# A hybrid encoder block on one core: attention values of two heads per 512-column product, and the recurrence's second output product issued earlier

## The chip, the cores and the metric

The kernel runs on one core of a Trainium2 chip. The time is the device time of one execution in microseconds (us); the median of several executions is the figure that counts. Everything is float32; TensorE does most products on float32 values split into a high and a low part.

## The reference

One layer of a trunk in which a differential attention and an RWKV-7 recurrence read the same normalised input and are merged by gates. 256 rows, width 2048, one layer:

```
h    = rmsnorm(x)
proj = h @ W_in                                  # q, k, v | r, k, v, low-rank columns | gate logits
A    = diff_attention(q, k, v)                   # 8 heads, each 2 x 128 for q and k, 256 for v
         p = softmax(q0 k0) - lam * softmax(q1 k1);  o = p @ v;  o = rmsnorm(o)
Bm   = rwkv7(...)                                # 32 heads of 64, per step:
         sa = state @ a;  state = state * w + sa b^T + v k^T;  y = state @ r
mix  = (sigmoid(gA) * (A @ W_a) + sigmoid(gB) * (Bm @ W_b)) @ W_out
x    = x + rmsnorm(mix)
x    = x + rmsnorm(swiglu(rmsnorm(x)))           # 2048 -> 2 x 5632 -> 2048
```

## The kernel before

Weights come from HBM in units of 128 x 1024 float32 (512 KB). `unit_parts` (lines 108 to 116) loads one into a `raw` tile (four buffers, issued on SP's queue), ACT copies it to a rounded high part `hi` (line 115), DVE subtracts to get the low part `lo` (line 116); `hi` and `lo` have four buffers each. `project_t` makes 128 output columns transposed, with the weights stationary: per 128 input columns one product of 512 columns (high weights, line 128) and one of 256 (low weights, line 131); ACT and DVE then add the two halves (`total`, lines 138 and 139). `project_rows` (lines 163 to 194) keeps the activations stationary and streams the weights: three products (high x high, high x low, low x high, line 177) per 128 input columns and per half of the 256 rows.

The first stage interleaves 16 groups of two recurrence heads (`rwkv_prep(g)`, lines 450 to 563) with 8 attention heads (`attention(h)`, lines 565 to 630) in the sequence `ORDER` (line 19): items 0 to 15 are groups, 100 to 107 are attention heads, and the list ends with 14, 15, 106, 107. A list scheduler with a simulated timeline then places each instruction on its engine's queue, so the written sequence is only a start; each queue runs strictly in its order.

`attention(h)` projects two q and two k parts with `project_t`, then the values of this head (256 columns): four units of weights, 96 products of 256 columns into one PSUM bank `va` whose two halves are the two row halves. ACT copies the bank to `vs[0]`, DVE subtracts to get `vs[1]` (lines 582 and 583). The scores (line 590) go to `mm` banks, softmax runs on ACT and DVE in a tile `pe`, line 605 transposes it, and line 613 multiplies by the values. PSUM has three `acc`, three `mm` and two `tr` banks.

`rwkv_prep(g)` ends with small products for a chunk's matrices (line 541, into two `mm` banks, read by DVE in line 544), and stores them to DRAM (`img`, `tl`). DVE then inverts 64 x 64 triangular matrices of eight groups at once (lines 390 to 396), which sit in `arena`: `inv_load(p)` (lines 384 to 388) is four loads from POOL's queue, each 8 rows of 16 KB (`arena<-tl`), and `inv_store` (lines 404 to 407) is two stores of 256 KB (`tx<-arena`). Loads for pair p = 4 and p = 5 are issued behind a step of groups 14 and 15; loads for p = 6 and p = 7 are issued behind the last q/k step of attention head 6 (lines 642 to 645).

Later, while the gate logits, `A @ W_a` and `Bm @ W_b` run, the recurrence proper is done in `chunk(p, c, ...)` (lines 696 to 736): 8 pairs p of groups times 4 chunks c. Each chunk has four small products per step, two heads into an `mm` bank and two into a `tr` bank, one on the upper and one on the lower 64 partitions: line 706 (full array), line 717 (64 x 64), line 723 (the next state's product), line 732 (the second part of the output Y). Between 717 and 723 DVE copies the state (720); behind 723 DVE adds or copies the next state from the bank (728, 730); behind 732 ACT copies Y out (736). In the profile each of these float32 products shows as two records.

Of the kernel before, what the change touches and what calls it, by code (L numbers as in the profile page):

```python
# [67 lines left out]
def hybrid_block(ctx: ExitStack, tc: tile.TileContext, io):  # L68
# [91 lines left out]
                    step_t(out, hi, lo, kk, xT, u * 8 + kk, nk)  # L160
        return [total(out) for out in outs]

    def project_rows(outs, src, base, xT, nk, width, banks_shared=False, tail=0):

        per = 1024 // width
        n = nk // per

        def part(u, j, hi, lo):
            for kk in range(per):
                k = u * per + kk  # L170
                wh, wl = hi[:, kk * width:(kk + 1) * width], lo[:, kk * width:(kk + 1) * width]
                for jj in j:
                    xh = xT[:, k, jj * P:(jj + 1) * P]
                    xl = xT[:, k, T + jj * P:T + (jj + 1) * P]
                    for i, (x, w) in enumerate(((xh, wh), (xh, wl), (xl, wh))):
                        first = k == 0 and i == 0 and (jj == 0 or not banks_shared)
                        mm = nc.tensor.matmul(outs[jj], lhsT=x, rhs=w, start=first,  # L177
                                              stop=(k == nk - 1 and i == 2 and (jj == 1 or not banks_shared)))
            return mm

        held = []
        for u in range(n):
            hi, lo = unit(src[base + u])
            if u < n - tail:
                mm = part(u, (0, 1), hi, lo)
            else:
                held.append((u, hi, lo))
        if tail:
            for u, hi, lo in held:
                mm = part(u, (0,), hi, lo)  # L190
            with tc.issue_after(mm.ins):
                for u, hi, lo in held:
                    mm = part(u, (1,), hi, lo)
        return mm
# [142 lines left out]
    with tc.tile_pool(name="hpool", bufs=1) as hpool:  # L337
# [42 lines left out]
        lt = arena[:, 0:4096].rearrange("p (s t) -> p s t", s=CH)  # L380
        xt = arena[:, 4096:6144].rearrange("p (j t) -> p j t", j=32)
        tmi = arena[:, 6144:7168]

        def inv_load(p):

# [23 lines left out]
        with tc.tile_pool(name="att", bufs=2) as w2, tc.tile_pool(name="mix1", bufs=2) as w1:  # L409
# [40 lines left out]
            def rwkv_prep(g):  # L450
# [111 lines left out]

                return after_kq, after_bkp

            def attention(h):
                def tmp(tag, shape=(P, T), bufs=2):
                    return w2.tile(list(shape), F32, tag=tag, name=tag, bufs=bufs)
                qk = []
                for i in range(4):
# [6 lines left out]
                    t = tmp(f"qk{i}", bufs=1)  # L576
                    after_qk = nc.gpsimd.tensor_tensor(out=t, in0=m1, in1=m2, op=ALU.add)
                    qk.append(t)
                va = bank("acc")
                project_rows([va[:, 0:256], va[:, 256:512]], io["w_inv"], 4 * h, hT, NK, 256, banks_shared=True)  # L580
                vs = [w2.tile([P, 2 * T], F32R, tag=f"vs{i}", name=f"vs{i}", bufs=1) for i in range(2)]
                nc.scalar.copy(vs[0], va)
                nc.vector.tensor_tensor(out=vs[1], in0=va, in1=vs[0].bitcast(F32), op=ALU.subtract)
                ptp = bank("tr")
                for qt in range(2):
                    nk = P * (qt + 1)
# [5 lines left out]
                    mx = tmp("mx", (P, 2))  # L592
                    nc.vector.tensor_reduce(out=mx, in_=s, axis=AX.X, op=ALU.max)
                    nc.vector.tensor_scalar(out=mx, in0=mx, scalar1=-SCALE, scalar2=None, op0=ALU.mult)
                    pe = tmp("pe", (P, 2, 256))
                    z = tmp("z", (P, 2))
                    for c in range(2):
                        nc.scalar.activation(pe[:, c, 0:nk], s[:, c], AF.Exp, scale=SCALE, bias=mx[:, c:c + 1], accum_out=z[:, c:c + 1])
# [11 lines left out]
                for q, pairs in enumerate(([(0, 0)], [(1, 0), (2, 1)])):  # L610
                    terms = [(a, b, i, j) for i, j in pairs for a, b in ((0, 0), (0, 1), (1, 0))]
                    for n, (a, b, i, j) in enumerate(terms):
                        nc.tensor.matmul(ob[:, q * T:(q + 1) * T], lhsT=pT[a][:, i * P:(i + 1) * P], rhs=vs[b][:, j * T:(j + 1) * T],
                                         start=(n == 0), stop=(n == len(terms) - 1))
                os_ = tmp("os", (P, 2, 256))
                ss = tmp("oss", (P, 2))
# [78 lines left out]
        with tc.tile_pool(name="chain", bufs=2, reuse_waits="tile") as cp:  # L695
            def chunk(p, c, ck, tb, y, nxt):
# [24 lines left out]
                if nxt is not None:  # L721
                    for g, h, o in heads:
                        nc.tensor.matmul(banks[h][own[h], 2 * P + o:2 * P + o + CH], lhsT=ckh[:, g, h, BKC:UVC], rhs=ckh[:, g, h, UVC:HW],
                                         start=True, stop=True, skip_group_check=True)
                    for h in range(2):
                        new = nxt[:, :, 0:ARC].rearrange("p g (h w) -> p g h w", h=2)[own[h], :, h, UVC:HW]
                        if c:
                            nc.vector.tensor_tensor(out=new, in0=part(banks[h][own[h]], 2), in1=st[own[h]], op=ALU.add)
                        else:
                            nc.vector.tensor_copy(new, part(banks[h][own[h]], 2))  # L730
                for g, h, o in heads:
                    nc.tensor.matmul(banks[h][own[1 - h], o:o + CH], lhsT=ck[own[h], g, ARC:IW], rhs=ckh[own[h], g, h, UVC:HW],  # L732
                                     start=False, stop=(g == 1), skip_group_check=True)
                yh = y[rows, c // 2].rearrange("p (g h e) -> p g h e", g=2, h=2)
                for h in range(2):
                    nc.scalar.copy(yh[:, :, h], part(banks[h][own[1 - h]], 0))
# [173 lines left out]
def prepare(x, w_in, b_gate, g_mix_pre, g_mix_post, g_ffn_pre, g_ffn_post, da_lambda_q, da_lambda_k, da_subln_g,  # L910
# [12 lines left out]
    for h in range(NH):  # L923
# [17 lines left out]
        "cst": _constants(),  # L941
        "vec": a(vec),
        "w_inb": a(_units_t(np.concatenate(cols, axis=1))),
        "w_inv": a(_units_rows(w[:, 4096:6144], 256)),
        "up_wa": a(np.concatenate([wu, au], axis=2).transpose(1, 0, 2)),
        "up_g": a(gu.transpose(2, 1, 0, 3).reshape(NG, P, 2 * P)),
        "w_ba": a(_units_t(np.asarray(w_branch_a)[0])),
# [21 lines left out]
```

## Time and profile before

| | |
|---|---|
| runs | 1996.11 us median of three (1995.98, 1996.11, 3871.28) |
| the profiled execution's own time | 1993.32 us |
| its span, first to last instruction | 1991.5 us |
| TensorE products (PE) busy | 1963.0 us, 99% |
| TensorE weight loads busy | 1698.6 us, 85% |
| DVE, ACT, POOL busy | 1354.0, 1026.3, 266.6 us |
| moved by DMA | 401.44 MB, mean 202 GB/s |

The stages follow one another: normalisation up to 25 us, recurrence preparation and attention up to about 680, gate logits, branch products and the recurrence up to 1153, `W_out` up to 1240, then the feed-forward layer. Busy time of PE is a modelled one for pipelined products, so what a product costs is read from the distance between starts.

### The profile page before, as it was taken

What the parts mean: (1) busy time and instruction counts of PE and PEld (TensorE: products, weight loads), DVE (VectorE), ACT (ScalarE), POOL (GpSimd) and SP (SyncE); (2) the same over time, 40 slices, a digit from 0 to 9 for tenths busy, and PEclk for the clock granted to TensorE, in tenths of its full rate; (3) what the DMA queues carried; (4) which work ended last, traced back from release to release, by engine and by line L of the source; (5) the groups of instructions that cost most, each with busy time, mean ns of one, the idle gap of its engine ahead of it and who ended that gap; (6) DMA issues with size and microseconds to landing.
All of it is one profiled execution on the core that took longest, in us unless ns stands there. A gap on an engine that the chain in (4) does not pass through costs nothing.

```text
span 1991.5 us, 32080 instructions
## 1 busy us (share of the span) xinstructions
PE 1963.0 (99%) x11934; PEld 1698.6 (85%) x11934; DVE 1354.0 (68%) x2173; ACT 1026.3 (52%) x1861; POOL 266.6 (13%) x359
## 2 busy tenths in 40 slices
PE   9999999999998999999999999999999999999998
PEld 8898899888887888888888888888888888888886
DVE  6767777899986888756656755656565656544444
ACT  6655655656664544445444444644444444434442
POOL 0224224133245111221110000000000000000000
PEclk9999999999999999999999999999999999999999
DMA  7677777765679675667546575555555555555664
GB/s 249 207 209 216 217 207 225 197 204 188 205 226 214 191 248 191 219 223 252 195 153 207 192 254 190 166 188 188 189 189 190 190 189 188 189 195 192 193 195 140
DMA packets 139307, 401.44 MB, mean 202 GB/s; under 512 B 32784, under 2 KB 45328, under 8 KB 138128
## 3 DMA queue, kind: packets, MB, share of 16 engines
q1 hardware_dynamic: 116432, 346.95, 54.5%
q0 software_dynamic: 12864, 45.10, 7.5%
q10 hardware_dynamic: 9856, 7.34, 1.2%
q8 instruction: 94, 1.54, 0.3%
q14 instruction: 61, 0.50, 0.1%
HBM read 368.92 MB, written 30.41 MB: 201 GB/s over the span
## 4 chain that ended last, share of the span: by engine, by line
PE 85%; DVE 6%; DMA 4%; issue 3%; ACT 1%; POOL 1%; DVEq 0%; SPq 0%; POOLq 0%; ACTq 0%
PE acc L128 39%; PE acc L131 20%; PE acc L177 18%; DMA raw<-w_inb 2%; DVE lo L116 2%; PE mm L206 1%; PE mm L706 1%; DVE arena L394 1%; PE tr L706 1%; DVE arena L396 1%; ACT hi L115 1%; PE mm L128 1%; PE mm L541 0%; PE tr L732 0%; PE tr L717 0%
## 5 line engine op out<-in xcount | busy, mean ns | idle before, releaser
L116 DVE TENSOR_TENSOR lo<-raw,hi 128x1024 fp32r<-128x1024 f32 x624 | 774.2, 1242 | 502.5 <-ACT hi L115 498.5
L115 ACT ACTIVATE hi<-raw 128x1024 fp32r<-128x1024 f32 x623 | 660.0, 1060 | 757.2 <-issue 313.8
L128 PE MATMUL acc<-hT,hi 128*128 128x512 f32 x1840 | 594.3, 400 | 0.0
L128 PE MATMUL acc<-h2T,hi 128*128 128x512 f32 x1392 | 439.3, 396 | 0.0
L131 PEld LDWEIGHTS acc<-hT,lo 128*128 128x128 f32 x1840 | 342.8, 188 | 76.7 <-DVE lo L116 1.6
L131 PE MATMUL acc<-hT,lo 128*128 128x256 f32 x1840 | 381.4, 284 | 0.6 <-DVE lo L116 0.5
L131 PEld LDWEIGHTS acc<-h2T,lo 128*128 128x128 f32 x1392 | 261.2, 188 | 60.6
L128 PEld LDWEIGHTS acc<-hT,hi 128*128 128x128 f32 x1840 | 285.6, 189 | 3.1 <-ACT hi L115 0.3
L131 PE MATMUL acc<-h2T,lo 128*128 128x256 f32 x1392 | 274.8, 278 | 0.0
L177 PE MATMUL acc<-hi,f 128*128 128x512 f32 x704 | 216.8, 389 | 0.0
L128 PEld LDWEIGHTS acc<-h2T,hi 128*128 128x128 f32 x1392 | 213.2, 189 | 0.8
L177 PEld LDWEIGHTS acc<-hi,f 128*128 128x128 f32 x704 | 132.2, 188 | 27.4
L177 PE MATMUL acc<-lo,f 128*128 128x512 f32 x352 | 136.9, 389 | 0.0
L229 POOL TENSOR_TENSOR rlastq<-rlast,mhalf 128x1 f32<-128x1 f32 x8 | 4.8, 606 | 942.5 <-DVE rlast L227 751.2
L139 DVE TENSOR_TENSOR sum<-acc,sum 128x256 f32<-128x256 f32 x233 | 97.3, 418 | 0.8
L177 PE MATMUL acc<-hi,hT 128*128 128x256 f32 x512 | 94.3, 283 | 0.0
L138 ACT COPY sum<-acc 128x256 f32<-128x256 f32 x233 | 83.7, 359 | 1.0 <-PE acc L128 0.3
L128 PE MATMUL acc<-oaT,hi 128*128 128x512 f32 x256 | 82.8, 399 | 0.0
L177 PEld LDWEIGHTS acc<-hi,hT 128*128 128x128 f32 x512 | 80.4, 191 | 0.0
L177 PE MATMUL acc<-hi,mixT 128*128 128x512 f32 x256 | 79.0, 389 | 0.0
L177 PEld LDWEIGHTS acc<-lo,f 128*128 128x128 f32 x352 | 66.1, 188 | 13.7
L128 PE MATMUL acc<-obT,hi 128*128 128x512 f32 x240 | 76.0, 395 | 0.0
(251 smaller groups left out, 2272.5 us busy)
## 6 DMA issues: line engine op xcount, KB each, us to landing
raw<-w_f SPq DMA_DIRECT2D x264, 512.0 KB, 3.5
raw<-w_inb SPq DMA_DIRECT2D x232, 512.0 KB, 4.1
ck<-img POOLq DMA_DIRECT2D x32, 576.0 KB, 5.9
raw<-w_inv SPq DMA_DIRECT2D x32, 512.0 KB, 4.0
raw<-w_ba SPq DMA_DIRECT2D x32, 512.0 KB, 3.6
raw<-w_bb SPq DMA_DIRECT2D x32, 512.0 KB, 3.5
raw<-w_out SPq DMA_DIRECT2D x32, 512.0 KB, 4.1
img<-stg POOLq DMA_DIRECT2D x32, 256.0 KB, 4.4
```

What stands on the lines that cost most here:

```text
L115: return (hi, lo, lambda: nc.scalar.activation(hi, raw, AF.Copy), lambda: nc.vector.tensor_tensor(out=lo, in0=raw, in1=hi.bitcast(F32), op ...
L116: lambda: nc.vector.tensor_tensor(out=lo, in0=raw, in1=hi.bitcast(F32), op=ALU.subtract), raw)
L128: nc.tensor.matmul(out, lhsT=hi[:, kk * P:(kk + 1) * P], rhs=xT[:, k, :], start=(k == 0), stop=(k == nk - 1))
L131: nc.tensor.matmul(out[:, 0:T], lhsT=lo[:, kk * P:(kk + 1) * P], rhs=xT[:, k, 0:T], start=False, stop=False)
L138: nc.scalar.copy(t, out[:, T:2 * T])
L139: nc.vector.tensor_tensor(out=t, in0=out[:, 0:T], in1=t, op=ALU.add)
L177: mm = nc.tensor.matmul(outs[jj], lhsT=x, rhs=w, start=first, stop=(k == nk - 1 and i == 2 and (jj == 1 or not banks_shared)))
L206: nc.tensor.matmul(out, lhsT=w[:, i:i + P], rhs=x, start=(n == 0), stop=(n == len(terms) - 1))
L229: nc.gpsimd.tensor_tensor(out=q, in0=r, in1=mhalf[:, 0:1], op=ALU.pow)
L394: nc.vector.tensor_tensor(out=tv, in0=xt[:, 0:n, s:s + 1].to_broadcast([P, n, m]), in1=lt[:, s:s + 1, s + 1:CH].to_broadcast([P, n, m]), o ...
L396: nc.vector.tensor_tensor(out=xt[:, 0:n, s + 1:CH], in0=xt[:, 0:n, s + 1:CH], in1=tv, op=ALU.add)
L706: nc.tensor.matmul(banks[h][:, o:o + CH], lhsT=ckh[:, g, h, 0:P], rhs=ckh[:, g, h, UVC:HW], start=(g == 0), stop=(g == 1))
```

## The change

Values: `attention(h)` projects values only when h is even, then for heads h and h + 1 together. The weights `w_inv` are laid out in units of 2 x 512 columns instead of 4 x 256, the two row halves take one `acc` bank each, and a product has 512 columns. The parts live in four tiles `vs00` to `vs11` until head h + 1 has used them. To make room, the softmax tile `pe` becomes a slice of `arena` (columns 7168 to 8191, otherwise unused). The argument `banks_shared` goes.

Recurrence: in `chunk`, the four products of the second part of Y (line 732 before, 730 after) are written directly behind the next state's products (723 before, 727 after), ahead of DVE's reading of that state.

```diff
-    def project_rows(outs, src, base, xT, nk, width, banks_shared=False, tail=0):
+    def project_rows(outs, src, base, xT, nk, width, tail=0):
...
-                        first = k == 0 and i == 0 and (jj == 0 or not banks_shared)
-                        mm = nc.tensor.matmul(outs[jj], lhsT=x, rhs=w, start=first,
-                                              stop=(k == nk - 1 and i == 2 and (jj == 1 or not banks_shared)))
+                        mm = nc.tensor.matmul(outs[jj], lhsT=x, rhs=w, start=(k == 0 and i == 0), stop=(k == nk - 1 and i == 2))
...
+        probs = arena[:, 7168:8192].rearrange("p (q c k) -> p q c k", q=2, c=2)
...
+            values = {}
...
-                va = bank("acc")
-                project_rows([va[:, 0:256], va[:, 256:512]], io["w_inv"], 4 * h, hT, NK, 256, banks_shared=True)
-                vs = [w2.tile([P, 2 * T], F32R, tag=f"vs{i}", name=f"vs{i}", bufs=1) for i in range(2)]
-                nc.scalar.copy(vs[0], va)
-                nc.vector.tensor_tensor(out=vs[1], in0=va, in1=vs[0].bitcast(F32), op=ALU.subtract)
+                if h % 2 == 0:
+                    va = [bank("acc"), bank("acc")]
+                    project_rows(va, io["w_inv"], 4 * h, hT, NK, 512)
+                    for j in range(2):
+                        values[j] = [w2.tile([P, 2 * T], F32R, tag=f"vs{j}{i}", name=f"vs{j}{i}", bufs=1) for i in range(2)]
+                        nc.scalar.copy(values[j][0], va[j])
+                        nc.vector.tensor_tensor(out=values[j][1], in0=va[j], in1=values[j][0].bitcast(F32), op=ALU.subtract)
...
-                    pe = tmp("pe", (P, 2, 256))
+                    pe = probs[:, qt]
...
-                        nc.tensor.matmul(ob[:, q * T:(q + 1) * T], lhsT=pT[a][:, i * P:(i + 1) * P], rhs=vs[b][:, j * T:(j + 1) * T],
+                        nc.tensor.matmul(ob[:, q * T:(q + 1) * T], lhsT=pT[a][:, i * P:(i + 1) * P], rhs=values[j][b][:, h % 2 * T:(h % 2 + 1) * T],
...
+                for g, h, o in heads:
+                    nc.tensor.matmul(banks[h][own[1 - h], o:o + CH], lhsT=ck[own[h], g, ARC:IW], rhs=ckh[own[h], g, h, UVC:HW],
+                                     start=False, stop=(g == 1), skip_group_check=True)
+                if nxt is not None:
                     for h in range(2):
...
                         else:
                             nc.vector.tensor_copy(new, part(banks[h][own[h]], 2))
-                for g, h, o in heads:
-                    nc.tensor.matmul(banks[h][own[1 - h], o:o + CH], lhsT=ck[own[h], g, ARC:IW], rhs=ckh[own[h], g, h, UVC:HW],
-                                     start=False, stop=(g == 1), skip_group_check=True)
...
-        "w_inv": a(_units_rows(w[:, 4096:6144], 256)),
+        "w_inv": a(_units_rows(w[:, 4096:6144], 512)),
```

The first place is TensorE's queue (PE) in the recurrence, early in the second pair's chunks; L128 and L131 are products of the large projections that run at the same time, `mm` and `tr` the two banks of a chunk. Before:

```order
L723 MATMUL mm<-ck 64x64 x2
L128 MATMUL acc<-hT,hi 128x512
L131 MATMUL acc<-hT,lo 128x256 x2
L128 MATMUL acc<-hT,hi 128x512 x2
L131 MATMUL acc<-hT,lo 128x256 x2
L128 MATMUL acc<-hT,hi 128x512 x2
L131 MATMUL acc<-hT,lo 128x256 x2
L732 MATMUL mm<-ck 64x64 x2
L732 MATMUL tr<-ck 64x64 x2
L706 MATMUL mm<-ck 128x64 x2
L723 MATMUL tr<-ck 64x64 x2
```

The same stretch of PE's queue after the change, where L727 is the next state's product and L730 the second part of Y:

```order
L128 MATMUL acc<-hT,hi 128x512 x2
L727 MATMUL mm<-ck 64x64
L727 MATMUL tr<-ck 64x64
L727 MATMUL mm<-ck 64x64
L727 MATMUL tr<-ck 64x64
L730 MATMUL mm<-ck 64x64
L730 MATMUL tr<-ck 64x64
L730 MATMUL mm<-ck 64x64
L730 MATMUL tr<-ck 64x64
```

The second part of Y left its own gaps between the large products and stands behind the state's products, with the two banks in turn. Over the whole queue the number of unbroken stretches that hold any of the 64 x 64 products falls from 101 to 68, and the number of groups of one line within them from 125 to 122.

The second place is POOL's queue at groups 14 and 15 and attention head 6. `arena<-tl` are the loads for the inversion (four to a pair p), `kq` and `bkp` steps of a group, `qk` the last step of a q or k part, `tx` the stores of the inverse. Before, from group 15's `kq` on:

```order
L496 TENSOR_TENSOR kq<-kr,mhalf 128x4
L388 DMA arena<-tl_85 8x4096 x4
L577 TENSOR_TENSOR qk_7495<-m_7490,m_7492 128x256
L388 DMA arena<-tl_85 8x4096 x4
L528 DMA bv_d<-sq 128x256
L517 TENSOR_TENSOR bkp<-bk,pt 128x512
L407 DMA tx_86<-arena 32x2048 x2
```

After, from group 14's second q/k step to group 15's loads:

```order
L527 DMA bv_d<-sq 128x256
L579 TENSOR_TENSOR qk_7195<-m_7190,m_7192 128x256
L387 DMA arena<-tl_85 8x4096 x4
L516 TENSOR_TENSOR bkp<-bk,pt 128x512
L406 DMA tx_86<-arena 32x2048 x2
L555 DMA img_83<-stg 64x4x64 x2
L559 DMA img_83<-stg 64x4x256
L560 DMA img_83<-stg 64x4x128
L559 DMA img_83<-stg 64x4x256
L560 DMA img_83<-stg 64x4x128
L495 TENSOR_TENSOR kq<-kr,mhalf 128x4
L387 DMA arena<-tl_85 8x4096 x4
```

The loads of p = 6 moved from behind those of p = 5 (one q/k step apart) to ahead of group 14's stores, so that the stores and a step of group 15 lie between the two sets of loads.

## Rows read from the trace of the kernel before

**Rows 1.** The page, its first part: busy time of each engine.

```profile
PE 1963.0 (99%) x11934; PEld 1698.6 (85%) x11934; DVE 1354.0 (68%) x2173; ACT 1026.3 (52%) x1861; POOL 266.6 (13%) x359
```

**Rows 2.** Busy time by stretch, columns in the first row.

```profile
core 0: us, PE busy (x) PEld busy (x) DVE busy (x) ACT busy (x) POOL busy (x), PEclk, DMA share, GB/s
...
600.00:680.00 80.00, 68.37 (x468) 62.15 (x467) 54.88 (x102) 34.36 (x68) 33.90 (x47) 0.94 0.86 208
...
860.00:960.00 100.00, 99.80 (x723) 82.50 (x722) 61.16 (x116) 52.68 (x116) 18.30 (x25) 1.00 0.67 225
```

**Rows 3.** The chain that ended last: start, us, what, number of products.

```profile
103.00 11.51 PE acc L177 x96
...
1153.93 72.10 PE acc L177 x318
```

**Rows 4.** Groups of line 177 in the value projections, by line.

```profile
L177 PE MATMUL acc<-hi,hT 128*128 128x256 f32 x512 | 94.3, 283 | 0.0
...
L177 PE MATMUL acc<-lo,hT 128*128 128x256 f32 x256 | 72.9, 285 | 0.0
```

**Rows 5.** Timeline of PE, 600 to 690: start, us, what, idle before and its releaser.

```profile
633.54 0.40 PE L131 MATMUL acc<-hT,lo 128*128 128x256 f32 x2
642.59 2.07 PE L590 MATMUL mm<-qk,qk 128*128 128x256 f32 x4 [8.65 <-DVE stg L544]
644.10 1.41 PE L128 MATMUL acc<-hT,hi 128*128 128x512 f32 x2
...
648.08 0.63 PE L128 MATMUL acc<-hT,hi 128*128 128x512 f32 x2
```

**Rows 6.** Timelines of DVE, ACT and POOL, 612 to 646.

```profile
640.71 1.23 DVE L116 TENSOR_TENSOR lo<-raw,hi 128x1024 fp32r<-128x1024 f32 x1 [10.61 <-ACT hi L115]
641.85 1.28 DVE L544 TENSOR_TENSOR stg<-mm,cst 128x512 f32<-128x512 f32 x2
...
639.62 1.06 ACT L115 ACTIVATE hi<-raw 128x1024 fp32r<-128x1024 f32 x1 [11.71 <-DMA raw<-w_inb]
...
617.01 2.10 POOL L388 DMA_DIRECT2D arena<-tl  x4
...
622.17 2.02 POOL L388 DMA_DIRECT2D arena<-tl  x4
```

**Rows 7.** The chain that ended last, 600 to 690.

```profile
621.67 17.85 DMA raw<-w_inb
```

**Rows 8.** DMA issues of the whole span: KB each, median us to landing.

```profile
raw<-w_inb SPq DMA_DIRECT2D x232, 512.0 KB, 4.1
...
arena<-tl POOLq DMA_DIRECT2D x32, 128.0 KB, 10.1
```

**Rows 9.** Timeline of PE in the recurrence, 722 to 760.

```profile
721.86 0.63 PE L128 MATMUL acc<-hT,hi 128*128 128x512 f32 x2
...
724.65 0.63 PE L128 MATMUL acc<-hT,hi 128*128 128x512 f32 x2
...
741.55 0.39 PE L128 MATMUL acc<-hT,hi 128*128 128x512 f32 x1
741.87 0.45 PE L723 MATMUL tr<-ck 128*64 128x64 f32 x4
742.24 0.44 PE L717 MATMUL tr<-w,tb 64*64 64x64 f32 x4
...
742.96 0.40 PE L131 MATMUL acc<-hT,lo 128*128 128x256 f32 x2
...
749.50 0.39 PE L128 MATMUL acc<-hT,hi 128*128 128x512 f32 x1
749.82 0.44 PE L732 MATMUL mm<-ck 64*64 64x64 f32 x4
...
750.54 0.40 PE L131 MATMUL acc<-hT,lo 128*128 128x256 f32 x2
```

**Rows 10.** Busy time in the stretch ahead of the stall, columns as in rows 2.

```profile
590.00:610.00 20.00, 20.00 (x132) 17.49 (x131) 16.52 (x32) 11.33 (x19) 10.19 (x13) 1.00 0.96 226
```

## Prediction

> **What bounds the kernel now.** I read the page first: PE is busy 99% of the span, DVE 68%, ACT 52% [rows 1]. With one engine so full, what counts is how much PE time the queue holds and where it stands still. So the second view is busy time by stretch: from 860 to 960, in the recurrence, PE has 99.80 of 100 us; the one large hole is between 600 and 680 with 68.37 of 80 us [rows 2]. In the same row the granted clock is 0.94, so part of that stretch ran at the lower of the two levels (1.2 instead of 2.4 GHz). Third came the chain, the PE timeline and the timelines of the other engines, for the price of a product and for the hole.
>
> **Values.** Before, 768 products of 256 columns (512 with a high and 256 with a low weight part) [rows 4]. The first block of 96 takes 11.51 us, 0.1199 each. `W_out` runs the same three products with 512 columns: 72.10 us for 318, 0.2267 each [rows 3]. After the change there are 4 blocks of 96 of these: 768 x 0.1199 = 92.1 us become 384 x 0.2267 = 87.1, a gain of 5.0. The other end comes from the gate projections beside it: 721.86 to 724.65 holds eight pairs of 512 and 256 columns, 0.349 a pair [rows 9]; if 512 columns cost two thirds of that, 0.2327, the gain is 2.7. I take 5.0, because `W_out` has the same pattern of products; ends 2.7 and 6 (a gain in the few interruptions of a block).
>
> The Trainium skill, in "TensorE: Matmul & The Clock Gate", section "Back-to-back issue gap", gives N / 2.4 ns plus 2.5 ns for N columns at full clock: 109.2 and 215.8 ns, so that two products of 256 cost only 2.5 ns more than one of 512. By that the gain would be 384 x 2.5 ns = 1.0 us, an estimate from that page. The rows here show 119.9 and 226.7 ns, 13.1 ns of difference per doubled product, and the sum goes by them.
>
> The rest of this edit I cost at nothing. The copies of the values are as many as before (ACT and DVE, two 128 x 512 each per head), and units of weights stay 32, so DVE and ACT have the same work per unit. A block now holds two of three `acc` banks for 96 x 0.2267 = 21.8 us, but on PE's new queue no product of a large projection stands inside a block, so nobody asks for the third meanwhile. The odd head loses 11.5 us of its own PE work between its q/k parts and its softmax; the scheduler puts the projections of the recurrence groups there. `pe` in `arena` touches columns nobody else uses and keeps two halves.
>
> **Recurrence.** What does a small group cost among large products? A group of line 732 alone: from the large product at 749.50 to the second next at 750.54 is 1.04 us, less two products of 512 (0.465) = 0.575. Two groups in one stretch: 741.55 to 742.96 is 1.41, less 0.465 = 0.945 [rows 9]. So a further group costs 0.37, and entering and leaving the stretch 0.575 - 0.37 = 0.205. The number of such stretches falls from 101 to 68, the number of groups from 125 to 122: 33 x 0.205 + 3 x 0.37 = 6.8 + 1.1 = 7.9 us. The ends: 3.4, if only half of entering and leaving is saved (33 x 0.10), and 12.2, if each stretch that goes takes its group's time along (33 x 0.37) because its records run beside those of the other bank.
>
> The edit also delays: DVE's reading of the next state now waits behind four more products, one group, 0.37 us. 24 chunks have a next state: 24 x 0.37 = 8.9 us if this were on the path, and the term would be a loss of 1.0. I take it as hidden, since PE has 99.80 of 100 us there [rows 2] and the chunks of two pairs overlap. Behind the waiting DVE instruction stand `lo` parts of weights, for which PE waits; they have up to four buffers of lead. In exchange PE's second part of Y no longer waits for DVE's reading, and ACT's copy of Y follows both.
>
> **The hole at 634.** The PE timeline: after 633.54 the next product starts at 642.59, a score product (line 590) that waited 8.65 us for DVE's line 544, which frees its `mm` bank [rows 5]. DVE's timeline: line 544 ran at 641.85, right behind a `lo` that had waited 10.61 us for ACT. ACT waited 11.71 us for a unit of weights [rows 6]. This transfer took 17.85 us [rows 7] where the median is 4.1 [rows 8], 13.75 us late. What crowds it are the loads of `arena<-tl`, 10.1 us each at a quarter of the size [rows 8]: two sets of four, issued at 617.01 and 622.17 [rows 6]. Then the clock: 644.10 to 648.08 holds six pairs of large products in 3.98 us [rows 5] instead of 6 x 0.349 = 2.09, so 1.9 us were lost at the lower level, after the engine had stood still. Together 8.65 + 1.9 = 10.5 us.
>
> On POOL's new queue these two sets no longer stand one q/k step apart: p = 6 goes ahead of group 14's stores, p = 5 comes a whole step of group 15 later. I price one set at half the lateness, 6.9 us; with one set in reach the stall is 8.65 - 6.9 = 1.8 us, and so short a pause need not cost the clock: a gain of 8.7. But the set of p = 6 falls into a stretch whose DMA share is already 0.96 [rows 10]. No PE time is lost there now (20.00 of 20.00), how much lead is left no row shows; the bounds are 0 and the whole set, 6.9, and I take 3.0, a little under the middle. The term is 5.7, with ends of 10.5 gained (the hole closes) and 6.9 lost (it stays and a set is added).
>
> **Sum.** 5.0 + 7.9 + 5.7 = 18.6 us. The profiled execution took 1993.32, so 1974.7; it stands 2.8 us under the median of the runs, 1996.11, so the prediction in terms of the median is 1977.5 us.
>
> **Rivals.**
> - The crowd of transfers only moves, and PE stands still as long as before, elsewhere. For it: all three sets and the stores still have to be moved in some 40 us with the DMA share at 0.96. Against it: the sets are further apart. Only the first two terms are left: 1996.1 - 12.9 = 1983.2; with one more set in the way 1990.1.
> - The recurrence gains nothing, because the state product that DVE waits for is late by the 0.37 us above and the order of the chunks is bound by that. For it: DVE reads the state after every one of these products. Against it: PE idles 0.2 us in 100. 1977.5 + 7.9 = 1985.4.
> - The value products cost by columns: the 0.1199 us holds a cost of this stretch that 512 columns would pay twice, 0.2398. For it: 512 columns have not been run in this stretch with this pattern. Against it: the same three products in `W_out`. 1977.5 + 5.0 = 1982.5. With the formula of the Trainium skill quoted above it would come to 1981.5.
> - Slower than before: the loads of p = 4, 6, 5 and 7 run into each other, and now meet value blocks of eight units in a row. Four sets are 4 x 6.9 = 27.5 us late; of that PE's lead absorbs what it absorbed before, 13.75 - 8.65 = 5.1, so PE stands 22.4 us, plus 1.9 of clock, 24.3, and with the two stores behind them, each priced as half a set, up to 31. Less the 10.5 of before and the 12.9 gained: 0.9 to 7.6 us slower, 1997.0 to 2003.7. It decides from a stall of about 22 us on. For it: p = 7 follows p = 5 closely in POOL's queue. Against it: p = 7 waits for group 15's own stores, and p = 4 is issued early.
>
> **How the numbers follow.** The forecast has 0.50, with a range of its own of 1967 to 1985 (the ends of the first two terms, and a stall between none and as now); the moved crowd 0.25, the recurrence without gain 0.10, values by column 0.07, slower 0.08. The range from 1964 (5 + 12.2 + 10.5 gained, and some 4 in the other holes) to 1998 leaves out most of the slower case and the far ends. All of these lie within 2% (40 us) of 1996.1, about what a measurement of this kernel can tell from no change: 0.96 for that; 0.03 for faster, since 40 us would need all terms at their far ends and more; 0.01 for slower.
>
> **What would show it.** In the profile after: L177's successor in a value block at 0.227 us from start to start with 512 columns, blocks of about 21.8 us, four of them; in the recurrence, the second part of Y directly behind the state's products and, among large products, 0.945 us for a stretch of two groups; PE still at 99 to 100 us of 100 in the recurrence. At groups 14 and 15, PE waits of under 5 us and a granted clock of 1.00; units of weights landing under 11 us after issue. The prediction is wrong in the first term if the distance is 0.24, in the second if DVE's reading of the state shows up as what PE waits for, in the third if a wait for `raw` of over 10 us remains in the chain, wherever it is.

## The result and the profile after

| | before | after |
|---|---|---|
| median of the runs | 1996.05 us | 1971.54 us (1970.18 to 1974.84, four runs) |
| ratio, 95% interval | | 0.9884, 0.987 to 0.9899 |
| the profiled execution's own time | 1993.32 us | 1970.18 us |
| its span | 1991.5 us | 1968.4 us |
| PE busy | 1963.0 us | 1945.4 us |

The kernel became 24.5 us faster (1.2%), 18.6 had been forecast (1977.5). The measured median lies in the range and below the forecast. One of the four runs of the kernel before took 3871.28 us, and the ratio is of the others. These others are few: against nine later runs of the kernel before (median 1993.06) the changed kernel, run again beside them, is 20.5 us faster (1972.56), so the gain is known to about 4 us.

The page after, its first part; it answers to [rows 1]:

```profile
PE 1945.4 (99%) x11550; PEld 1673.5 (85%) x11550; DVE 1348.1 (68%) x2173; ACT 1026.3 (52%) x1861; POOL 268.7 (14%) x359
```

384 records fewer on PE, and 17.6 us less busy time; the busy time of DVE, ACT and POOL has moved by at most 6 us. The chain of the changed kernel and its groups by line, which answer to [rows 3] and [rows 4] (line 176 is the former 177):

```profile
103.95 21.80 PE acc L176 x96
```

```profile
L176 PE MATMUL acc<-hi,hT 128*128 128x512 f32 x256 | 81.8, 394 | 0.0
...
L176 PE MATMUL acc<-lo,hT 128*128 128x512 f32 x128 | 50.7, 396 | 0.0
```

384 products of 512 columns, in the first block 21.80 / 96 = 0.2271 us each. Four such blocks would take 87.2 us where eight of 11.51 would have taken 92.1: 4.9 us, and 5.0 had been priced. Only this first block stands in one piece. In the other three, small products of the recurrence groups stand between the value products, and they last 24.1, 24.6 and 30.7 us from start to end (the last with a stall and slow clock inside); in the kernel before too, blocks were interrupted. Added up over the blocks ahead of 500 us that kept the full clock, a product took 0.2300 us after (288 of them) and 0.1209 before (480), which gives 4.5 us for all. So the term is an estimate of 4.5 to 4.9.

Busy time by stretch after, columns as in [rows 2]:

```profile
0.00:25.00 25.00, 20.79 (x201) 18.07 (x201) 13.71 (x37) 16.30 (x36) 3.51 (x10) 1.00 0.76 266
...
600.00:680.00 80.00, 72.10 (x397) 60.99 (x396) 53.95 (x105) 35.34 (x71) 32.09 (x44) 0.96 0.89 211
...
860.00:960.00 100.00, 100.00 (x753) 84.32 (x752) 63.11 (x122) 54.27 (x123) 19.17 (x28) 1.00 0.70 234
```

In the recurrence PE has 100.00 of 100 us. Between 600 and 680 it stands for 7.90 us instead of 11.63, and the granted clock is 0.96 instead of 0.94: the hole is smaller, not closed. The clock, in finer stretches, first the kernel before, then two stretches of the changed kernel:

```profile
630.00:650.00 20.00, 11.35 (x53) 9.55 (x52) 7.54 (x18) 4.92 (x10) 5.58 (x7) 0.74 0.88 214
```

```profile
610.00:630.00 20.00, 16.43 (x85) 13.37 (x84) 7.42 (x11) 8.35 (x20) 6.50 (x10) 0.91 0.96 234
...
650.00:670.00 20.00, 20.00 (x110) 17.51 (x111) 15.45 (x31) 10.25 (x21) 11.33 (x16) 0.93 0.91 224
```

Before, about half of the time at the lower level (1.2 GHz) fell into the stall itself, where it costs nothing; PE was busy for 5.2 us of it. After, the clock fell at both of the shorter stalls, and PE was busy for 5.9 us at the lower level. So the higher mean gave no time back.

What PE waits for after, the largest waits (us in total, times, longest):

```profile
PE mm L252 <- DVE xn L246: 3.7, 3, 1.8
PE mm L594 <- DVE stg L543: 3.7, 1, 3.7
PE tr L531 <- ACT stg L548: 3.6, 1, 3.6
```

One stall of 8.65 us [rows 5] has become two of 3.7 and 3.6, one at group 14 and one at group 15. DVE's reading of the next state is not among them. The first of the three is the normalisation at the start, which the change does not touch; PE stands there 1.8 us longer in this execution (20.79 of 25 us busy against 22.57), and less so in the next profile of the same kernel below.

The chain of the changed kernel between 560 and 700, which answers to [rows 7]:

```profile
604.62 19.05 DMA raw<-w_inv
...
631.76 13.29 DMA raw<-w_inb
...
656.58 11.39 DMA raw<-w_inb
```

Units of weights are as late as before, now three times in the chain, and yet PE stood for less time behind them; no row shows why.

The recurrence after: one chunk's state and Y products in one stretch. The timeline of PE, 723 to 725; L727 is the state's product, L730 the second part of Y:

```profile
723.44 0.63 PE L128 MATMUL acc<-hT,hi 128*128 128x512 f32 x2
723.90 0.28 PE L131 MATMUL acc<-hT,lo 128*128 128x256 f32 x1
724.11 0.27 PE L727 MATMUL mm<-ck 128*64 128x64 f32 x1
724.12 0.27 PE L727 MATMUL tr<-ck 128*64 128x64 f32 x1
...
724.49 0.27 PE L730 MATMUL mm<-ck 64*64 64x64 f32 x1
...
724.87 0.39 PE L131 MATMUL acc<-hT,lo 128*128 128x256 f32 x1
725.09 0.62 PE L128 MATMUL acc<-hT,hi 128*128 128x512 f32 x2
```

From 723.44 to 725.09 are 1.65 us; two pairs of large products (0.698) taken off, the stretch of two groups costs 0.952, where [rows 9] gave 0.945. The two banks' records go in turn (724.11, 724.12).

To compare whole recurrences I added up, in the trace of each kernel, the distances from start to start of the chunks' small products and of what the large products between them take over 0.2327 (512 columns) and 0.1163 (256), from the first product of a chunk to the last transpose of Y. That sum is 116.3 us before and 103.3 after: 13.0 us gained, where the prediction had 7.9. 0.7 us of the 13.0 is time in which PE stood idle in the recurrence before. So the profiled execution's 23.1 us are 4.5 to 4.9 for the values, 13.0 in the recurrence, and 4.9 of idle time less before 680 (18.05 us in the windows before, 13.17 after); 0.3 to 0.7 us is left over.

### The profile page after: what moved, and what is told of

Same layout as the page of the kernel before. It is cut to its first block, busy times and chain, and to the rows that moved or that the text cites. A ratio compares the mean times of both kernels' runs of the same rounds, so it can differ in the third digit from the quotient of the medians.

```text
span 1968.4 us, 31263 instructions
## 1 busy us (share of the span) xinstructions
PE 1945.4 (99%) x11550; PEld 1673.5 (85%) x11550; DVE 1348.1 (68%) x2173; ACT 1026.3 (52%) x1861; POOL 268.7 (14%) x359
## 4 chain that ended last, share of the span: by engine, by line
PE 92%; DMA 3%; DVE 2%; issue 1%; ACT 1%; POOL 1%; POOLq 0%; DVEq 0%; SPq 0%; ACTq 0%
PE acc L128 43%; PE acc L131 22%; PE acc L176 18%; DMA raw<-w_inb 1%; PE mm L204 1%; DMA raw<-w_inv 1%; PE tr L710 1%; PE mm L710 1%; DVE lo L116 1%; PE mm L540 1%; PE mm L128 1%; PE mm L730 1%; ACT hi L115 1%; PE mm L594 0%; PE mm L727 0%
## 5 line engine op out<-in xcount | busy, mean ns | idle before, releaser
L128 PE MATMUL acc<-hT,hi 128*128 128x512 f32 x1840 | 592.1, 399 | 0.0
L128 PE MATMUL acc<-h2T,hi 128*128 128x512 f32 x1392 | 439.3, 396 | 0.0
L131 PEld LDWEIGHTS acc<-hT,lo 128*128 128x128 f32 x1840 | 343.2, 188 | 76.0 <-DVE lo L116 0.7
L131 PE MATMUL acc<-hT,lo 128*128 128x256 f32 x1840 | 379.2, 283 | 0.0
L131 PEld LDWEIGHTS acc<-h2T,lo 128*128 128x128 f32 x1392 | 261.2, 188 | 60.6
L128 PEld LDWEIGHTS acc<-hT,hi 128*128 128x128 f32 x1840 | 285.1, 189 | 2.5 <-DVE vs L587 0.4
L131 PE MATMUL acc<-h2T,lo 128*128 128x256 f32 x1392 | 274.8, 278 | 0.0
L128 PEld LDWEIGHTS acc<-h2T,hi 128*128 128x128 f32 x1392 | 213.2, 189 | 0.8
L128 PE MATMUL acc<-oaT,hi 128*128 128x512 f32 x256 | 83.3, 400 | 0.0
L176 PE MATMUL acc<-hi,hT 128*128 128x512 f32 x256 | 81.8, 394 | 0.0
L128 PE MATMUL acc<-obT,hi 128*128 128x512 f32 x240 | 76.0, 395 | 0.0
L393 DVE TENSOR_TENSOR arena<-arena 128x462 f32<-128x462 f32 (+46 forms) x126 | 66.9, 531 | 3.4 <-issue 2.0
```

Of the source, the lines that this page charges most:

```text
L128: nc.tensor.matmul(out, lhsT=hi[:, kk * P:(kk + 1) * P], rhs=xT[:, k, :], start=(k == 0), stop=(k == nk - 1))
L131: nc.tensor.matmul(out[:, 0:T], lhsT=lo[:, kk * P:(kk + 1) * P], rhs=xT[:, k, 0:T], start=False, stop=False)
L176: mm = nc.tensor.matmul(outs[jj], lhsT=x, rhs=w, start=(k == 0 and i == 0), stop=(k == nk - 1 and i == 2))
L393: nc.vector.tensor_tensor(out=tv, in0=xt[:, 0:n, s:s + 1].to_broadcast([P, n, m]), in1=lt[:, s:s + 1, s + 1:CH].to_broadcast([P, n, m]), o ...
```

## The experiments

The first four ran together on one chip, the last four on another occasion; the kernel before took 1993.33 us in the first series and 1993.06 in the second. Theory at the start: the sum of three separate terms, of which the recurrence's is due to the number of stretches. Rivals: that the edits depend on each other, that DVE's reading of the state counts, and that the crowd of transfers only moves.

**One part alone.** The changed kernel with Y written behind DVE's reading again, as before:

```diff
-                for g, h, o in heads:
-                    nc.tensor.matmul(banks[h][own[1 - h], o:o + CH], lhsT=ck[own[h], g, ARC:IW], ...
                 if nxt is not None:
                     for h in range(2):
...
+                for g, h, o in heads:
+                    nc.tensor.matmul(banks[h][own[1 - h], o:o + CH], lhsT=ck[own[h], g, ARC:IW], ...
```

> The kernel after the change with the recurrence written as before (second part of Y behind DVE's reading of the next state); the first stage is instruction for instruction that of the changed kernel, and 92 unbroken stretches hold 64 x 64 products (101 before, 68 after). Theory of three separate terms: values 4.9 us, holes of the first stage about 7 us, and nine stretches fewer, 9 x 0.205 = 2 us: 1982 us, within 4. Rival, that the recurrence edit pays nothing and all of the 24.5 us lies in the first stage: 1971 to 1974 us.

Measured: 1982.67 us, ratio 0.995 (0.9935 to 0.9964), 10.7 us faster than before. That lies where the three separate terms put it (1982), and the rival of this run (1971 to 1974) is out. The recurrence's sum is 114.4, so 1.9 us of it come there, from another order of the same products (92 stretches instead of 101). The values' part and a smaller hole are the rest. That sum hides something, as a wait of PE in this run shows, where L737 is the second part of Y and L733 DVE's addition to the next state:

```profile
PE tr L737 <- DVE ck L733: 1.5, 2, 1.0
```

In this execution Y stood behind DVE's reading of the state for 1.5 us, and after the longer of the two waits the clock fell to the lower level, at which PE worked for 6.8 us (half of it, 3.4 us, lost). Without the two the sum would be 109.5: the other order of the unchanged code alone is worth some 6 to 7 us of the recurrence, and this wait is one that the edit of the recurrence takes away.

The other part alone: the kernel before with the reverse edit, Y directly behind the state's products.

> The kernel before with only the second part of Y moved; the first stage is instruction for instruction that of before, with its hole of 8.65 us, and 69 stretches instead of 101. Theory: only entering and leaving stretches and the groups in them change, 32 x 0.205 = 6.6 us by the prediction's price and some 12 us by the difference of the two traces: 1984 to 1989 us, below 1986 if the trace is right. Rival (the order of the chunks is bound by DVE's later reading of the state): 1995 to 1998 us.

Measured: 1979.11 us, ratio 0.9934 (0.9921 to 0.9947), 14.2 us faster, which is below the range that I had expected (1984 to 1989). Its recurrence costs 103.7 us, as in the changed kernel, with 69 stretches. The hole stays, as its waits of PE and the stretch show:

```profile
PE mm L590 <- DVE stg L544: 7.5, 2, 6.8
```

```profile
600.00:680.00 80.00, 71.02 (x477) 64.74 (x476) 55.92 (x105) 34.88 (x69) 33.39 (x46) 0.94 0.85 212
```

The first stage is the same as in the kernel before, and PE stands there for 8.98 us instead of 11.63: the hole swings by 2.7 us between two executions of the same instructions.

10.7 + 14.2 = 24.9 beside 24.5 for both against the first runs, and 20.5 against the later ones; each of these has an interval of about 3 us either way, and within it the parts add up. The recurrence's part is the larger, and larger than I had priced it.

**Y first.** The changed kernel with Y written ahead of the next state's products instead of behind them, so that the state comes one group later:

```diff
+                for g, h, o in heads:
+                    nc.tensor.matmul(banks[h][own[1 - h], o:o + CH], lhsT=ck[own[h], g, ARC:IW], ...
                 if nxt is not None:
                     for g, h, o in heads:
                         nc.tensor.matmul(banks[h][own[h], 2 * P + o:2 * P + o + CH], ...
-                for g, h, o in heads:
-                    nc.tensor.matmul(banks[h][own[1 - h], o:o + CH], lhsT=ck[own[h], g, ARC:IW], ...
```

> The changed kernel with the second part of Y written ahead of the next state's products instead of behind them: both still stand together (72 stretches, 68 after), but the state comes one group, 0.37 us, later on PE as well. Theory of stretches: as the changed kernel, 1971.5 us plus at most 2. Rival (what pays is that the state's product goes first and DVE starts early): 24 x 0.37 = 8.9 us slower, 1980 us.

Measured: 1976.16 us, ratio 0.9919 (0.9905 to 0.9932), 17.2 us faster than before. That is 4.6 us above 1971.5, more than the 2 that I had allowed, and under the 1980 of the rival. Its recurrence costs 105.9 us, 2.6 more than the changed kernel's, with 72 stretches and 127 groups against 68 and 122: 4 x 0.205 + 5 x 0.37 = 2.7. So the count agrees with this part; the other 2 us are no more than the runs scatter (the profiled execution, 1981.7 us, was the slowest of the five and stood longer in the first stage). The other theory's 8.9 us would be on top of the 2.7 and are not there: in the recurrence PE has no idle time in this trace (340.00 of 340 us from 720 to 1060), so the later state is hidden.

**The loads of p = 6 alone.** The kernel before with these four loads issued behind head 6's second q/k step, where the changed kernel has them:

```diff
-                        with tc.issue_after(after_qk.ins):
+                        with tc.issue_after(second.ins):
                             inv_load(6)
+                        with tc.issue_after(after_qk.ins):
                             inv_load(7)
```

> The kernel before, with the four loads of p = 6 for the inversion issued behind the second q/k step of attention head 6 instead of the fourth, which is where the changed kernel's POOL queue has them; values and recurrence as before. If the changed place of these loads is what shortened the hole: the stall of 8.65 us falls under 5 and the time to 1989 to 1993 us. Rival (the hole shrank because value blocks of eight units stand there): stall and time as before, 1996 us within 2.

Measured: 1994.47 us, ratio 1.0002 (0.999 to 1.0015): no change. Its waits of PE and the stretch:

```profile
PE tr L532 <- ACT stg L549: 5.1, 1, 5.1
...
PE acc L177 <- DVE lo L116: 3.1, 1, 3.1
PE tr L627 <- ACT os L623: 3.1, 1, 3.1
```

```profile
600.00:680.00 80.00, 68.77 (x466) 63.13 (x465) 55.52 (x103) 34.11 (x69) 34.32 (x47) 0.94 0.86 209
```

The stall of 8.65 us at the score product is gone, and three others stand in its place: 68.77 us busy beside 68.37, the clock 0.94 as before. Moving these loads moves the hole. That was a rival of the prediction, and of this edit by itself it is true.

**Again.** The changed kernel once more, for comparison with the next three:

> The changed kernel as it is, beside the next three, so that they are compared with it on the same chip. Both theories: 1969 to 1975 us, 20 to 27 us under the kernel before; PE waits of 3 to 5 us each for DVE's stg and for ACT's stg around groups 14 and 15 appear again.

Measured: 1972.56 us, ratio 0.99 (0.9885 to 0.9916), 20.5 us faster than before in this series. Its two waits are 4.2 and 3.0 us, and in the first 25 us PE has 21.90, so between these two executions the hole's and the start's numbers swing by about 1 us.

**What a group costs.** By now I thought that the missing 5 us of the recurrence lay in groups of the two banks, one on the upper and one on the lower partitions, that run beside each other. This kernel writes state and Y of the one bank, then of the other:

```diff
-                if nxt is not None:
-                    for g, h, o in heads:
...
-                for g, h, o in heads:
...
+                for h in range(2):
+                    if nxt is not None:
+                        for g in range(2):
+                            nc.tensor.matmul(banks[h][own[h], 2 * P + g * CH:2 * P + g * CH + CH], ...
+                    for g in range(2):
+                        nc.tensor.matmul(banks[h][own[1 - h], g * CH:g * CH + CH], ...
```

> The changed kernel with the next state's products and the second part of Y written bank by bank (state, Y of the one bank, then state, Y of the other). By the order of PE's queue: 71 unbroken stretches with 64 x 64 products instead of 68, and 144 groups of one line instead of 122. Theory: what counts is entering and leaving a stretch (0.205 us), and a group on one half of the partitions runs beside the one on the other half, so groups by line are not the unit: 3 x 0.205 = 0.6 us more, within 2.5 us of the changed kernel on the same chip. Rival: each further group of a line costs its 0.37 us, as the prediction's term has it: 22 x 0.37 + 0.6 = 8.7 us more, at least 6.

Measured: 1982.06 us, ratio 0.9946 (0.9933 to 0.996), 9.5 us more than the changed kernel in the same series. In the traces 8.0 of it lie in the recurrence. The rival's 8.7 is about right, and my theory fell. Its timeline of PE (L728 the state's product, L731 Y):

```profile
741.68 0.63 PE L128 MATMUL acc<-hT,hi 128*128 128x512 f32 x2
742.24 0.45 PE L728 MATMUL mm<-ck 128*64 128x64 f32 x4
742.61 0.44 PE L731 MATMUL mm<-ck 64*64 64x64 f32 x4
742.98 0.45 PE L728 MATMUL tr<-ck 128*64 128x64 f32 x4
743.36 0.44 PE L731 MATMUL tr<-ck 64*64 64x64 f32 x4
...
745.22 0.50 PE L131 MATMUL acc<-hT,lo 128*128 128x256 f32 x2
745.57 0.62 PE L128 MATMUL acc<-hT,hi 128*128 128x512 f32 x2
```

The changed kernel at the same point of the program:

```profile
739.19 0.63 PE L128 MATMUL acc<-hT,hi 128*128 128x512 f32 x2
739.75 0.27 PE L727 MATMUL mm<-ck 128*64 128x64 f32 x1
...
740.13 0.27 PE L730 MATMUL mm<-ck 64*64 64x64 f32 x1
...
741.27 0.50 PE L131 MATMUL acc<-hT,lo 128*128 128x256 f32 x2
741.61 0.62 PE L128 MATMUL acc<-hT,hi 128*128 128x512 f32 x2
```

Both hold the state and Y of two chunks. Bank by bank there are eight groups of four records, 0.37 us from one start to the next, and 3.89 us in all; with the banks in turn four groups of eight records, 0.38 us from 739.75 to 740.13, and 2.42 us in all. A group costs 0.37 whether it holds one bank or both, and each return to a line is paid again.

**The crowd of transfers.** The changed kernel without the call `inv_load(6)` (the inversion of that pair then works on what stood in `arena`):

> The changed kernel without the four loads of arena for pair p = 6 (2 x 128 KB x 2; the inversion of that pair works on what stood in arena). Theory: these loads, issued at 607 into a stretch whose DMA engines are full, make the units of weights 13 to 19 us late, and PE then stands 3.6 us for ACT's stg at 626 and 3.7 us for DVE's stg at 650, and loses up to 3.4 us of slow clock: the first of the two waits falls under 1 us, the longest raw transfer of 600 to 680 under 14 us, and the time is 2 to 8 us under the changed kernel on the same chip. Rival: the stores of groups 14 and 15 and the other sets crowd the engines as much: both waits and the time stay within 1.5 us.

Measured: 1968.57 us, ratio 0.9877 (0.9863 to 0.989), 4.0 us less than the changed kernel. The waits:

```profile
PE mm L594 <- POOL qk L579: 3.6, 1, 3.6
PE mm L594 <- DVE stg L543: 2.2, 1, 2.2
```

The wait for ACT's `stg` is gone, the one for DVE's is 2.2, and units of weights between 595 and 665 land in at most 12.9 us instead of 19.8; a wait for POOL's `qk`, 0.5 us in the changed kernel's first profile, has become the largest. This is what I had expected of the theory. The recurrence stands in another order there and costs 106.2 us, 2.4 more, which the time contains, and POOL's queue has another order as well. So these four loads have a share in the stall, but are not the whole of it.

**Fewer and larger loads.** The changed kernel with the rows of the inversion laid out anew, so that a pair's load is two transfers of 16 rows instead of four of 8:

```diff
-            for r in (p % 4 * 8, 32 + p % 4 * 8):
-                for q in range(2):
-                    nc.gpsimd.dma_start(out=lt[q * 64 + r:q * 64 + r + 8], in_=tl_d[p // 4][r:r + 8])
+            r = p % 4 * 16
+            for q in range(2):
+                nc.gpsimd.dma_start(out=lt[q * 64 + r:q * 64 + r + 16], in_=tl_d[p // 4][r:r + 16])
...
-                for h in range(2):
-                    r = q * 64 + h * 32
-                    nc.gpsimd.dma_start(out=tx_d[b][:, q, h], in_=xt[r:r + 32])
+                for m in range(4):
+                    for h in range(2):
+                        r = q * 64 + m * 16 + h * 8
+                        nc.gpsimd.dma_start(out=tx_d[b][m * 8:m * 8 + 8, q, h], in_=xt[r:r + 8])
...
-                tl = tl_d[g // 8].rearrange("(h p g c) s t -> h s p g c t", h=2, g=2, c=NC)[:, :, g % 8 // 2, g % 2]
+                tl = tl_d[g // 8].rearrange("(p h g c) s t -> h s p g c t", h=2, g=2, c=NC)[:, :, g % 8 // 2, g % 2]
```

> The changed kernel with the rows of the inversion laid out so that a pair's load is two transfers of 16 rows of 16 KB instead of four of 8, the same bytes; its stores become eight of 8 rows per half instead of two of 32. Theory: a load of 8 rows occupies few of the DMA engines for long, and units of weights behind it on these engines are late; 16 rows spread it: arena<-tl still at about 10 us or less each for twice the size, the longest raw transfer of 600 to 680 under 14 us, the two PE waits of 3.6 us together under 4, and 2 to 7 us under the changed kernel. Rival: the bytes count and not their rows: waits and time as in the changed kernel, or up to 4 us more from the eight stores.

Measured: 1964.92 us, ratio 0.9863 (0.9849 to 0.9877), 7.6 us less than the changed kernel in the same series, a little more than the 2 to 7 of the theory. The DMA issues of the loads, first in the changed kernel, then here:

```profile
arena<-tl POOLq DMA_DIRECT2D x32, 128.0 KB, 9.7
```

```profile
arena<-tl POOLq DMA_DIRECT2D x16, 256.0 KB, 8.4
```

Its largest wait of PE, and the stretch:

```profile
PE mm L541 <- DVE bk L514: 2.3, 1, 2.3
```

```profile
600.00:680.00 80.00, 77.68 (x442) 66.83 (x441) 63.08 (x120) 41.59 (x87) 33.79 (x49) 0.98 0.83 234
```

A transfer of twice the bytes lands in less time. There are half as many of them, so for a pair's 512 KB the gain is smaller: from the first issue to the last landing they take 9.8 us in the median of the eight pairs, in the changed kernel 13.1. Units of weights between 595 and 665 take 5.7 us in the median and 13.1 at most, in the changed kernel's second profile 11.0 and 19.8, and PE has 77.68 us there where that one has 72.65. The rival, that waits and time stay because the bytes are the same, did not come. But the edit changes two more things: the stores are eight of 64 KB instead of two of 256 KB, and POOL's queue has another order. Since moving the loads brought nothing by itself (the fourth run), the size of the transfers is the likelier cause, but that is not shown: the three were not run apart. Its recurrence costs 106.4 us, 2.6 more than in the changed kernel: the gain in the first stage is larger than the 7.6.

By the Trainium skill, "DMA: Bandwidth & Descriptors", section "Why a DMA increments its semaphore by 16 and not by 1", a transfer is spread over the largest number of engines up to 16 that divides the outer dimension of both its sides: by that rule 8 for a load of 8 rows and 16 for one of 16. The times agree with it (128 KB in 9.7 us, 256 KB in 8.4); no row shows which engines moved what.

## Why the prediction was right, and where not

The total came close to the forecast although the recurrence was priced 5.1 us too low and the hole's term rests on a step that failed; as far as the hole goes, that is luck. The range that goes with the forecast, 1967 to 1985, has a slow end that does not follow from the ends it names: 1996.1 - 2.7 - 3.4 is 1990.

**Values: right.** 0.2271 us a product measured in the first block, 0.2267 taken, 4.5 to 4.9 us against 5.0. `W_out` was the right row to go by; the price by column (0.2398) is refuted. That four blocks would last about 21.8 us held for one of them: the small interruptions remained, which the prediction had allowed for as a gain. The gap formula quoted in the prediction from the Trainium skill gives 1.0 us for this term and does not hold here: two products of 256 cost 239.8 ns and one of 512 costs 227.1. The Trainium skill itself ("TensorE: Matmul & The Clock Gate", section "Back-to-back issue gap") gives it for an isolated product and says that in a stream of weight loads and products the spacing is another.

**Recurrence: right mechanism, term too small.** The part "33 x 0.205" is about right. What the large products take over their own time fell by 6.5 us (19.06 to 12.60), with 6.8 predicted: 0.19 us per stretch in both kernels, a little less before if the 0.5 us of standing idle in it is taken off. The Trainium skill, "TensorEngine Tiling (Array Packing)", section "Key Properties", has a rule for it: a change of tiling mode drains TensorE. The trace agrees in that each stretch has such a price; that it is a drain, no row shows.

The failed step is "3 x 0.37", the 1.1 us for groups. Groups are not all alike, which I had read off two examples. Some products of the kernel before stand as a group of 12 records, one bank's chunk with the other pair's two banks behind it. The timeline of PE in the kernel before, 800 to 802:

```profile
800.62 0.62 PE L128 MATMUL acc<-hT,hi 128*128 128x512 f32 x2
801.08 0.28 PE L131 MATMUL acc<-hT,lo 128*128 128x256 f32 x1
801.29 0.39 PE L723 MATMUL mm<-ck 128*64 128x64 f32 x3
801.46 0.27 PE L723 MATMUL tr<-ck 128*64 128x64 f32 x1
...
801.69 0.28 PE L723 MATMUL mm<-ck 128*64 128x64 f32 x2
801.90 0.39 PE L131 MATMUL acc<-hT,lo 128*128 128x256 f32 x1
```

It lasts from 801.29 to 801.90, 0.61 us, and was counted as one group of 0.37. There are 20 of these before (12.2 us) and 9 after (5.5); the other groups went from 38.4 to 40.8 us. Together the groups of 64-partition products gained 4.3 us instead of 1.1. Two more things were in no term. The full-array products of line 706 (of the kernel before) cost 0.59 us between two such groups and 0.36 among large products, and they stand at 31 such borders instead of 51: 1.8 us. And 0.5 us went with the products of line 206, another step's, that stand between them. 6.5 + 4.3 + 1.8 + 0.5 is 13.1, beside the 13.0 of the whole sum. That the edit brings this, and not the values, the two half kernels show: the recurrence alone has 12.6 us less and 9 of the groups of 12 records, the values alone 1.9 us less (some 6 to 7 without its wait and its slow clock) and 22 of them. So part of the gain can also come from another order of the unchanged code; the whole of it came only with the edit.

The 13.0 lie above even the upper end, 12.2. That had been given for another reason (records running beside those of the other bank), and the bank-by-bank run refutes that reason for groups one behind another.

The 8.9 us for DVE's later reading of the state were rightly taken as hidden: no wait of PE names it, PE has 100.00 of 100 us, and delaying the state by one more group cost what its groups cost.

**The hole: size not settled, reason wrong.** 5.7 us were priced. In 600 to 680 PE's idle time fell by 3.7 us in the profiled pair. But it swings: 11.63 and 8.98 us in the two profiles of the first stage of before, 7.35 to 9.59 in the five of the changed one, which overlap. By the medians, the 10.7 us of the values alone, less 1.9 in the recurrence and up to 4.9 for the products, leave about 4, known to about 3. The clock gave nothing (5.2 us of work at the lower level before, 5.9 after). And the step "I price one set at half the lateness, 6.9 us" failed: a unit of weights lands 19.05 us after its issue, not under 11. The next step, that so short a pause need not cost the clock, had nothing to stand on then: pauses of 3.6 and 3.7 us were left, not one of 1.8, and the clock is not 1.00. The chain has waits for `raw` of over 10 us, by which I had called this term wrong. Moving the loads as in POOL's new queue, without the rest, gave nothing. Why the changed kernel then stands for less time there, if it does, is not settled; its value blocks stand at other points of the queue, and that was not run apart. The rival of the moved crowd is thus right about the transfers; its time (1983.2) did not come, most of all because the recurrence gained more. The one of four sets running into each other did not come: PE stood for 7.3 us in two pieces, far from the 22 from which it decides.

## What to carry to other kernels

Where small products on part of the array stand between large ones, each unbroken stretch and each return to a line has a price of its own (here 0.2 and 0.37 us), so products that are ready at about the same time belong together, both halves of the partitions in turn; price them from all kinds of groups that the timeline holds, not from the first two. Where a stall comes from crowded transfers, moving one of them can just move the stall, as here; looking at how long a transfer of few rows takes for its bytes led to an edit that gave 7.6 us, though not to a proof that the rows were the cause. And a stall of a few us has to be read from more than one execution before a gain in it is believed.

## What the runs showed that I had not expected

- A group of 64-partition products takes 0.373 us from start to start with the four records of one bank and 0.380 with the eight of both in turn: the second half of the array costs nothing, but only record by record. Even another line's product joins for nothing. In the timeline of the changed kernel, Y of one pair goes in turn with line 721 of another, 12 records between 768.28 and 769.57. 1.29 us less 0.698 is 0.59, which is what a group alone costs with entering and leaving its stretch (0.575 in the prediction):

```profile
768.28 0.63 PE L128 MATMUL acc<-hT,hi 128*128 128x512 f32 x2
768.84 0.27 PE L730 MATMUL mm<-ck 64*64 64x64 f32 x1
768.85 0.27 PE L730 MATMUL tr<-ck 64*64 64x64 f32 x1
768.86 0.27 PE L721 MATMUL tr<-w,tb 64*64 64x64 f32 x1
...
769.57 0.40 PE L128 MATMUL acc<-hT,hi 128*128 128x512 f32 x1
```

- Four loads of 128 KB with 8 rows each stand beside 512 KB units of weights that are 15 us late (19.05 for a unit of `w_inv` against a median of 3.7; 12.9 at most without the loads of p = 6). With 16 rows to a load, a transfer of 256 KB took 8.4 us where one of 128 KB took 9.7, and a pair's set of loads 9.8 us instead of 13.1.
